# Five of six weight products of a unit and token block issued as two matmuls of 256 columns

## The chip, the cores and the metric

The kernel runs on one core of one Trainium2 chip. The metric is the time of one execution on the device in microseconds (us), and the median of several runs is compared. Every time below comes from such runs or from one execution that the hardware profiler recorded.

## The reference, cut to what matters

The computation is a decoder trunk of two layers on 256 tokens with a model width of 2048, all in 32-bit floats. Layer 0 has a combined input projection (2048 to 6160), stick-breaking attention beside gated linear attention, and an output projection (2048 to 2048). Layer 1 has a diagonal state-space mixer and a gated projection (2048 to 4096). Both layers end in a SwiGLU feed-forward part (2048 to 11264, then 5632 to 2048), and every part has norms before and after it:

```python
for layer in range(DEPTH):
    y = rms_norm(h, g[0])
    y = sb_gla_mixer(y, ...) if layer % 2 == 0 else s5_mixer(y, ...)
    h = h + rms_norm(y, g[1])
    y = swiglu_ffn(rms_norm(h, g[2]), w_ffn_in[layer], w_ffn_out[layer])
    h = h + rms_norm(y, g[3])
```

Nearly all of the arithmetic is the product of 256 tokens with these weight matrices, some 360 MB of weights that are each read once.

## The kernel before

**Splitting a product.** A weight product in full 32-bit precision is made of three products in the type fp32r, which TensorE streams at one pass. Activations and weights are each split into a high part and a low remainder; the kernel adds activation high times weight high, activation high times weight low, and activation low times weight high. ScalarE (ACT) makes the high part of a weight by a rounding copy and VectorE (DVE) makes the low part by a subtraction (`Stream.convert`, line 108).

**Tiles.** The output is made in blocks of 512 columns, and each block has two token blocks of 128 tokens, each of which adds up in one PSUM bank of 128 x 512 floats. Weights come from memory by the SP queue in chunks of 512 rows by 512 columns (1 MB); half a chunk, 256 rows, is a *unit*. `linear` (line 208) and `pairwise` (line 265) loop over the column blocks and, within one, over the units; for each unit they fetch its split weights (`ws.next`), call `products` (line 192) for token block 0 and for token block 1, and then let `pump` (line 171) issue some background work for DVE and ACT by the planner's costs.

**A call of `products`.** It handles one unit for one token block: two row blocks `kk` of 128 rows, and for each of them the three products of lines 203, 204 and 205. In the call of the matmul the activations (128 rows by 128 tokens) are the stationary operand, which TensorE has to load first (LDWEIGHTS, the engine PEld in the profile), and the weights (128 rows by 512 columns) stream past them. Each of these six matmuls has its own load. The first matmul of an output block carries the flag `start`, which clears the bank, and the last carries `stop`, after which ACT and DVE read the bank. A few chunks of layer 1 have no low part and go through plain 32-bit matmuls on line 198 instead.

**Order.** The schedule is written by hand: TensorE's instructions stand in the order in which the code issues them, and an instruction waits for what it reads. The converter runs `ahead` units (3 or 4) in front of TensorE. Between units the background work may put transposes or small matmuls of the mixers into TensorE's order (lines 337, 480, 734, 810, 923 to 954, 1233, 1414 to 1490).

**How many.** The stream holds 48 chunks of the input projection, 16 of the output projection, 176 and 88 of the feed-forward parts and 32 of the gated projection: 360 chunks, of which 4 go through line 198. The other 356 are 712 units. There are 92 column blocks (12, 4, 68 and 8), so 184 accumulations with one first and one last matmul each.

Of the kernel before, what the change touches and what calls it, by code (L numbers as in the profile page):

```python
# [159 lines left out]
class Kern:  # L160
# [31 lines left out]
    def products(self, ps, acts, tb, u, part):  # L192
        hi, lo = part
        mm = self.nc.tensor.matmul
        if lo is None:
            for kk in range(2):
                k = 2 * u + kk
                mm(ps, lhsT=self.whole[k][:, tb * 128:(tb + 1) * 128], rhs=hi[:, kk, :], start=(k == 0), stop=(k == len(acts) - 1))  # L198
            return
        for kk in range(2):  # L200
            k = 2 * u + kk
            xh, xl = (a[:, tb * 128:(tb + 1) * 128] for a in acts[k])
            mm(ps, lhsT=xh, rhs=hi[:, kk, :], start=(k == 0), stop=False)  # L203
            mm(ps, lhsT=xh, rhs=lo[:, kk, :], start=False, stop=False)  # L204
            mm(ps, lhsT=xl, rhs=hi[:, kk, :], start=False, stop=(k == len(acts) - 1))  # L205


    def linear(self, blocks, acts, evac, opening=None, mid=None, hooks=None, spare=None):
# [497 lines left out]
    def gla(self, rs):  # L706
# [86 lines left out]
        yield from self.need(256)  # L793
        mix = self.got.pop(256)
        yield from products(S[1], mix, mix, 0, 128, lambda o, p: nc.vector.tensor_copy(o, p))
        for li, b in enumerate((64, 32, 16, 8, 4, 2, 1)):
            yield from self.need(2 * b + 1)
# [805 lines left out]
```

## Time and profile before

| what | value |
|---|---|
| time, median of 3 runs | 2204.62 us (2203.36 to 2204.85) |
| the profiled execution's own time | 2204.35 us |
| its span, first to last instruction | 2202.6 us |
| mean granted TensorE clock | 0.996 |
| PE busy (matmul) | 2159.6 us, 98% of the span, 10672 instructions |
| PEld busy (loads of the stationary operand) | 1741.4 us, 79%, 10672 instructions |
| DVE busy | 1319.5 us, 60% |
| ACT busy | 974.3 us, 44% |
| mean rate of the DMA queues | 208 GB/s |

A matmul's row in the profile lasts longer than its share of the engine, because matmuls overlap in the pipeline: the row of a 512-column matmul is some 396 ns long, while the next begins some 232 ns after it. What a matmul costs is therefore read from the distance between starts. In a row, `128*128 128x512 f32` means 128 rows by 128 columns of stationary operand and 512 streamed columns; a plain 32-bit matmul appears as two rows, one for each of its passes. PEclk is the granted clock as a share of full speed.

### The profile page before, as it was taken

To read this page: it belongs to the slowest core of one execution; us is meant where nothing else is said; L and a number is where in the kernel's file an instruction comes from. 1 tells how busy PE (TensorE), PEld (TensorE's weight loads), DVE (VectorE), ACT (ScalarE), POOL (GpSimd) and SP (SyncE) were. 2 spreads that over 40 slices of the span, in tenths; PEclk is the share of its full clock that TensorE was granted. 3 is DMA by queue.
4 is the path that set the end of the run, shared out by engine and by line. 5 is a ranking of instruction groups with operands and counts; after the bars stand their busy time and mean duration, and the time that the engine had idled before them with its cause. 6 is when DMAs were issued, how large, how long until landed. Compare 5 with 4: busy or idle time off the path is not lost.

```text
span 2202.6 us, 26942 instructions
## 1 busy us (share of the span) xinstructions
PE 2159.6 (98%) x10672; PEld 1741.4 (79%) x10672; DVE 1319.5 (60%) x1913; ACT 974.3 (44%) x1222; POOL 7.1 (0%) x14
## 2 busy tenths in 40 slices
PE   8999999999999999999998899999999999999998
PEld 6888888788888888777786678878888888888886
DVE  4675654667777877875456864564544454444445
ACT  5454544463454444334344254464434444433433
POOL 0000000000000000000000000000000000000000
PEclk9999999999999999999999999999999999999999
DMA  7554454555687778988769865645555555555553
GB/s 230 171 176 156 159 173 155 206 190 175 202 268 236 241 221 267 300 275 275 238 214 349 305 209 185 213 170 176 195 183 191 191 173 190 174 206 174 191 172 134
DMA packets 261742, 457.42 MB, mean 208 GB/s; under 512 B 22736, under 2 KB 66016, under 8 KB 260720
## 3 DMA queue, kind: packets, MB, share of 16 engines
q1 hardware_dynamic: 260896, 450.99, 62.0%
q0 software_dynamic: 720, 4.72, 0.6%
q8 instruction: 83, 1.36, 0.2%
q14 instruction: 43, 0.35, 0.0%
HBM read 425.26 MB, written 30.41 MB: 207 GB/s over the span
## 4 chain that ended last, share of the span: by engine, by line
PE 94%; DVE 3%; ACT 1%; DMA 1%; issue 0%; SPq 0%; DVEq 0%; ACTq 0%
PE lin L203 29%; PE lin L205 29%; PE lin L204 29%; PE lin L198 1%; PE big L480 1%; DVE h L65 1%; DVE X L65 0%; PE big L810 0%; DVE wlo L65 0%; ACT xh L65 0%; PE big L1233 0%; PE big L205 0%; PE big L204 0%; PE big L203 0%; DVE xl L65 0%
## 5 line engine op out<-in xcount | busy, mean ns | idle before, releaser
L65 DVE TENSOR_TENSOR wlo<-wraw,whi 128x1024 fp32r<-128x1024 f32 x705 | 850.3, 1222 | 591.1 <-ACT whi L65 588.8
L65 ACT CAST whi<-wraw 128x1024 fp32r<-128x1024 f32 x705 | 725.3, 1051 | 670.7 <-PE lin L205 609.2
L203 PE MATMUL lin<-whi,xh 128*128 128x512 f32 x1984 | 790.6, 398 | 3.4 <-ACT xh L65 3.4
L204 PE MATMUL lin<-wlo,xh 128*128 128x512 f32 x1984 | 785.1, 396 | 3.0 <-DVE wlo L65 2.9
L205 PE MATMUL lin<-whi,xl 128*128 128x512 f32 x1984 | 784.9, 396 | 0.9 <-DVE xl L65 0.9
L203 PEld LDWEIGHTS lin<-whi,xh 128*128 128x128 f32 x1984 | 374.9, 189 | 91.2 <-ACT xh L65 4.0
L204 PEld LDWEIGHTS lin<-wlo,xh 128*128 128x128 f32 x1984 | 374.8, 189 | 90.4 <-DVE wlo L65 6.0
L205 PEld LDWEIGHTS lin<-whi,xl 128*128 128x128 f32 x1984 | 374.5, 189 | 88.7 <-DVE xl L65 2.2
L203 PE MATMUL lin<-whi,ah 128*128 128x512 f32 x680 | 270.0, 397 | 0.0
L205 PE MATMUL lin<-whi,al 128*128 128x512 f32 x680 | 268.9, 395 | 0.0
L204 PE MATMUL lin<-wlo,ah 128*128 128x512 f32 x680 | 268.9, 395 | 0.0
L203 PEld LDWEIGHTS lin<-whi,ah 128*128 128x128 f32 x680 | 128.1, 188 | 30.8 <-issue 1.2
L205 PEld LDWEIGHTS lin<-whi,al 128*128 128x128 f32 x680 | 128.1, 188 | 30.3
L204 PEld LDWEIGHTS lin<-wlo,ah 128*128 128x128 f32 x680 | 128.1, 188 | 30.0
L65 DVE SCALAR_TENSOR_TENSOR a<-lin,rs,a 128x512 f32<-128x512 f32 x44 | 31.0, 746 | 67.3 <-PE lin L205 67.3
L65 ACT ACTIVATE a<-lin,rs 128x512 f32<-128x512 f32 x44 | 27.9, 684 | 92.2 <-PE lin L205 92.2
L65 DVE TENSOR_TENSOR yg<-lin,yg 128x512 f32<-128x512 f32 x30 | 19.9, 687 | 52.1 <-PE lin L205 52.1
L65 ACT ACTIVATE junk<-yg 128x512 f32<-128x512 f32 x24 | 15.2, 632 | 74.1 <-DVE yg L65 74.1
L65 ACT CAST ah<-big 128x1024 fp32r<-128x1024 f32 x22 | 22.3, 1015 | 56.2 <-PE big L480 56.2
L65 DVE TENSOR_TENSOR al<-big,ah 128x1024 fp32r<-128x1024 f32 x22 | 26.9, 1223 | 17.1 <-ACT ah L65 17.1
L65 ACT ACTIVATE xh<-big,gT 128x128 fp32r<-128x128 f32 (+1 forms) x80 | 24.3, 394 | 21.5 <-PE big L337 16.9
L65 DVE SCALAR_TENSOR_TENSOR xl<-big,gT,xh 128x128 fp32r<-128x128 f32 (+1 forms) x80 | 24.5, 371 | 13.6 <-ACT xh L65 13.6
(323 smaller groups left out, 1287.1 us busy)
## 6 DMA issues: line engine op xcount, KB each, us to landing
wraw<-w_ffn_in SPq DMA_DIRECT2D x176, 1024.0 KB, 5.1
wraw<-w_ffn_out SPq DMA_DIRECT2D x88, 1024.0 KB, 5.5
wraw<-w_in SPq DMA_DIRECT2D x47, 1024.0 KB, 5.0
wraw<-w_glu SPq DMA_DIRECT2D x32, 1024.0 KB, 5.7
wraw<-w_out SPq DMA_DIRECT2D x16, 1024.0 KB, 5.1
e_d<-ed SPq DMA_DIRECT2D x64, 144.0 KB, 5.9
et<-e_d SPq DMA_DIRECT2D x16, 576.0 KB, 6.3
win_d<-win SPq DMA_DIRECT2D x32, 256.0 KB, 6.6
```

The source lines that it names most:

```text
L65: return f(*a, **k)
L198: mm(ps, lhsT=self.whole[k][:, tb * 128:(tb + 1) * 128], rhs=hi[:, kk, :], start=(k == 0), stop=(k == len(acts) - 1))
L203: mm(ps, lhsT=xh, rhs=hi[:, kk, :], start=(k == 0), stop=False)
L204: mm(ps, lhsT=xh, rhs=lo[:, kk, :], start=False, stop=False)
L205: mm(ps, lhsT=xl, rhs=hi[:, kk, :], start=False, stop=(k == len(acts) - 1))
L480: nc.tensor.transpose(p[:, tb, i, :], a[:, tb, i * 128:(i + 1) * 128], self.ident)
```

## The change

The three products of a row block become a list of terms, and each term is issued either whole (512 columns) or as two matmuls of 256 columns each, which write the two halves of the bank and stream the two halves of the weights. Both halves use the same stationary operand. Whole stay the first term of the first row block of a unit (`kk == 0 and i == 0`, which includes the one with `start`), and the matmul with `stop`. So a call issues 11 matmuls in place of 6, or 10 where it holds the last one of an accumulation. The order of the sums in each output element is the same. Loads, conversions, transfers, the reading of the banks and the plain 32-bit path on line 198 are as they were.

```diff
         for kk in range(2):
             k = 2 * u + kk
             xh, xl = (a[:, tb * 128:(tb + 1) * 128] for a in acts[k])
-            mm(ps, lhsT=xh, rhs=hi[:, kk, :], start=(k == 0), stop=False)
-            mm(ps, lhsT=xh, rhs=lo[:, kk, :], start=False, stop=False)
-            mm(ps, lhsT=xl, rhs=hi[:, kk, :], start=False, stop=(k == len(acts) - 1))
+            terms = ((xh, hi), (xh, lo), (xl, hi))
+            for i, (x, w) in enumerate(terms):
+                start, stop = k == 0 and i == 0, k == len(acts) - 1 and i == 2
+                whole = stop or (kk == 0 and i == 0)
+                for c in (slice(0, 512),) if whole else (slice(0, 256), slice(256, 512)):
+                    mm(ps[:, c], lhsT=x, rhs=w[:, kk, c], start=start, stop=stop)
```

## The prediction

> **What bounds the kernel now.** I read the page first: the busy shares, then the chain of work that ended last, then the costliest groups.
>
> ```profile
> span 2202.6 us, 26942 instructions
> PE 2159.6 (98%) x10672; PEld 1741.4 (79%) x10672; DVE 1319.5 (60%) x1913; ACT 974.3 (44%) x1222; POOL 7.1 (0%) x14
> PE 94%; DVE 3%; ACT 1%; DMA 1%; issue 0%; SPq 0%; DVEq 0%; ACTq 0%
> PE lin L203 29%; PE lin L205 29%; PE lin L204 29%; PE lin L198 1%; PE big L480 1%; DVE h L65 1%; DVE X L65 0%; PE big L810 0%; DVE wlo L65 0%; ACT xh L65 0%; PE big L1233 0%; PE big L205 0%; PE big L204 0%; PE big L203 0%; DVE xl L65 0%
> ```
>
> TensorE sets the end: 94% of the chain is PE, 87% of it the three lines of the change. So what matters is how fast TensorE passes from one matmul to the next. The timeline of TensorE and its loads shows that (start in us, length in us):
>
> ```profile
> 600.17 0.39 PE L203 MATMUL lin<-whi,xh 128*128 128x512 f32 x1
> 600.40 0.40 PE L204 MATMUL lin<-wlo,xh 128*128 128x512 f32 x1
> 600.40 0.19 PEld L205 LDWEIGHTS lin<-whi,xl 128*128 128x128 f32 x1
> 600.63 0.40 PE L205 MATMUL lin<-whi,xl 128*128 128x512 f32 x1
> 600.63 0.19 PEld L203 LDWEIGHTS lin<-whi,xh 128*128 128x128 f32 x1
> ...
> 611.33 0.39 PE L203 MATMUL lin<-whi,xh 128*128 128x512 f32 x1
> ```
>
> Line 203 starts at 600.17 and again at 611.33, 48 matmuls later (16 times the three lines in turn): 11.16 us / 48 = **232.5 ns** from one whole matmul to the next. The load of the next stationary operand starts together with the matmul before it (600.40, 600.63) and its row is 0.19 us long, so it is done before that matmul ends.
>
> The other engines leave room where the work is densest (busy us of PE, PEld, DVE and ACT, then PEclk, DMA share and GB/s):
>
> ```profile
> 480.00:1180.00 700.00, 700.00 (x3260) 562.97 (x3260) 487.12 (x838) 296.58 (x346) 0.29 (x1) 1.00 0.77 242
> 1440.00:2180.00 740.00, 738.05 (x3231) 598.86 (x3230) 364.56 (x366) 312.01 (x362) 0.53 (x1) 1.00 0.54 182
> ```
>
> In these two stretches DVE is busy for 487 of 700 us and 365 of 740, and the DMA engines for 0.77 and 0.54 of the time, so a TensorE that is a few per cent faster is still fed. Should one of them be late next, it is DVE, whose low part of a unit is made in one piece:
>
> ```profile
> L65 DVE TENSOR_TENSOR wlo<-wraw,whi 128x1024 fp32r<-128x1024 f32 x705 | 850.3, 1222 | 591.1 <-ACT whi L65 588.8
> ```
>
> That is 1.22 us for a unit on which TensorE works for 12 x 232.5 ns = 2.79 us, so it hides with room of more than half.
>
> **The change part by part.** A unit and token block has six products. The stream has 712 split units (356 chunks by 2) and two token blocks: 712 x 2 x 6 = 8544 whole matmuls. At 232.5 ns they fill 1986 us, 90% of the span, which agrees with the chain's 87%. Whole stay 1424 firsts (712 x 2) and 184 lasts (92 column blocks x 2): 8544 - 1424 - 184 = **6936 products are cut in two**. That removes 6936 matmuls of 512 columns and adds 13872 of 256, each with its own load of 128 columns; so 6936 loads are added too. One ns on a cut product is 6.94 us. No wait is added: a half reads the same tiles and the `stop` matmul, on which the readers of the bank wait, stays single.
>
> What one half costs is not in the trace as such: an fp32r matmul of 256 columns with 128 loaded columns. Three rows stand around it. The nearest in type and length is line 734, fp32r too and 256 columns, but with a load of 16 columns:
>
> ```profile
> L734 PE MATMUL big<-xh,wlr_split 128*16 128x256 f32 x32 | 5.7, 278 | 0.6 <-ACT wlr_split L65 0.4 <-DVE wlr_split L65 0.2
> 46.42 0.28 PE L734 MATMUL big<-xl,wlr_split 128*16 128x256 f32 x1
> ...
> 50.84 0.28 PE L734 MATMUL big<-xl,wlr_split 128*16 128x256 f32 x1
> ```
>
> The low product comes once in three there, so 13 x 3 = 39 matmuls lie between these two rows: 4.42 us / 39 = **113.3 ns**. Two of them are 226.7, which is 5.8 ns less than a whole one. The second row is the nearest in the load: line 810, a plain 32-bit product, whose passes of 128 columns run at half the rate and take as much stream as 256 columns of fp32r, each with a load of 128 columns. Beside it I put line 198, the same kind with 512 columns:
>
> ```profile
> 182.92 1.95 PE L810 MATMUL big<-qd,de 128*128 128x128 f32 x16
> 182.92 1.76 PEld L810 LDWEIGHTS big<-qd,de 128*128 128x128 f32 x15
> L810 PE MATMUL big<-qd,de x112: 273/276/276, 118.3 to 197.5; 128*128 128x128 f32 x112
> 1259.79 2.74 PE L198 MATMUL lin<-wraw,y 128*128 128x512 f32 x6
> L198 PE MATMUL lin<-wraw,y x64: 592/593/697, 1249.4 to 1281.8; 128*128 128x512 f32 x64
> ```
>
> Sixteen rows of line 810 in 1.95 us, the last 276 ns long: (1950 - 276) / 15 = **111.6 ns** from one to the next. So TensorE takes a load of 128 columns every 111.6 ns beside a stream of that length: the load fits under a half of 113.3 ns, with less than 2 ns to spare. Line 198: (2740 - 593) / 5 = 429.4 ns.
>
> Does the load slow the stream, so that twice as many loads cost more? One row speaks against it: a 512-column matmul behind which no load ran.
>
> ```profile
> 427.60 0.39 PE L204 MATMUL big<-hl,os 128*128 128x512 f32 x1
> 427.61 0.19 PEld L205 LDWEIGHTS big<-hl,os 128*128 128x128 f32 x1
> 427.83 0.40 PE L205 MATMUL big<-hl,os 128*128 128x512 f32 x1
> 429.22 0.42 PEld L337 LDWEIGHTS big<-ident,h 128*128 128x128 f32 x4 [1.43 <-DVE xl L65]
> ```
>
> The matmul of 427.83 has no load beside it until 429.22, and its row is 0.40 us, as long as that of 427.60, which has one. So the load is not what makes 512 columns cost more than twice 113.3 ns. What does, the trace does not say: the length itself, or the 128 output columns where line 734 has 16.
>
> The cost of a half is thus bounded from below by 111.6 ns (the load has no room under it), and from above by the case that all that a whole fp32r matmul has over its ideal is paid per instruction. Half of line 198's pass, 429.4 / 2 = 214.7, is that ideal for 512 columns; 232.5 - 214.7 = 17.8 ns is the surplus, and a half would be 107.35 + 17.8 = 125.2 ns. I take **114.0**: the row of the same type and length, 113.3, and 0.7 for a load that is tight against it (112 of 113). Two halves are 228.0, which is 4.5 ns less than 232.5; 6936 x 4.5 = **31 us** less. Nothing else enters the sum. The other terms at nothing: more instructions to hand out, since line 1233 hands out a pair of load and matmul every 25 ns, (650 - 279) / 15, and more to fetch, which is 1.36 of 457 MB moved:
>
> ```profile
> 1010.12 0.65 PE L1233 MATMUL big<-et 128*32 128x128 f32 x16
> L1233 PE MATMUL big<-et 128*32 128x128 f32 x256 | 10.3, 279 | 0.0
> DMA packets 261742, 457.42 MB, mean 208 GB/s; under 512 B 22736, under 2 KB 66016, under 8 KB 260720
> ...
> q8 instruction: 83, 1.36, 0.2%
> ```
>
> If hiding fails there, each of the 6936 pairs costs what it is late by. The sum stands against the profiled execution's own 2204.35 us (its span of 2202.6 and 1.75 around it): 2204.35 - 31.2 = 2173.1. The median of the runs is 0.27 us above that execution, so **2173 us** stands for both.
>
> A rule of the Trainium skill speaks against the change. TensorE: Matmul & The Clock Gate, section Back-to-back issue gap, gives 518 cycles for 512 columns and 262 for 256 at full clock, so by it two halves cost 6 cycles more than one, an estimate of 2.5 ns, or 17 us more in all (2222). The trace has 232.5 and 113.3 ns where that page has 216 and 109, so the excess that the page does not know is on the long matmul; the measurement decides, and the rule's sign lives on in the first rival.
>
> **The rivals.**
>
> *A fixed price per matmul* (slower). Four matmuls of 128 columns on line 810 are 446.4 ns, one of 512 on line 198 is 429.4: three more matmuls and loads cost 17.0 ns, 5.7 each. If fp32r streams at a rate of its own that goes by the column (232.5 for 512), a cut product costs 232.5 + 5.7: 6936 x 5.7 = 39 us more, 2243. It happens at the hand-over between two halves, and it decides from a half of 116.6 ns on. For it: both rows are firm, and a load that starts with the matmul before it has only the half's length. Against it: line 734 hands over 39 times at 113.3, less than half of 232.5. At the far end of the same place lies the whole surplus of 17.8 per matmul: 6936 x 17.8 = 123 us, 2328; line 734, with 6 ns over its ideal, speaks against that.
>
> *The rate goes by the column and the hand-over is free* (no change). If 2.2 columns per ns is simply what fp32r does with 128 output columns, a half is 116.25 and two are 232.5: 2204. For it: the row without a load is as long as the others, so the surplus sits in the stream. Against: 113.3 on line 734.
>
> *The change does more than the row* (faster still). With halves at 111.6, the bound of the load, the gain is 9.3 x 6936 = 65 us, 2140. Nothing shows fp32r streaming faster than line 734, so I give this little.
>
> **How the numbers follow.** My forecast, halves between 112.5 and 115.9 ns, has 0.50; its own range is 2153 to 2200. No change, within 0.2% (4.4 us, 0.3 ns on a half; about what a measurement of this kernel can tell), has 0.13. The fixed price at some 5.7 ns has 0.26, and its far end, towards 2328, 0.08. Still faster has 0.03. Together: faster 0.53, same 0.13, slower 0.34. The range goes down to 2150, which leaves out the last case, and up to 2290, which is 85.7 / 6.936 = 12.4 ns on a cut product or a half of 122.4 ns, well past the fixed price of 5.7 and short of its far end; with that end about 0.1 is left out in all, a little less than it might be, since no row shows the half itself.
>
> **What would show it.** In the changed kernel the groups of the split line have the form 128x256 with a mean near 278 ns, as on line 734 (near 282 if the rate goes by the column), and 13872 of them; two matmuls of 256 start 228 ns apart from the next two in the timeline. The load rows come 114 ns apart and PEld is busy for nearly all of the span. The whole matmuls stay at 232.5. PE waits and DVE's busy time stay as they are. The prediction is wrong if halves start over 116.25 ns apart; if then the load's rows start late, after the matmul before them, the load is the bound, and if the matmul rows are longer than 282 ns it is the stream.

## The result

The changed kernel is slower: 2229.5 us against 2204.49, medians of 4 runs each. The ratio is **1.0117**, 95% interval 1.0099 to 1.0134. That is 25.0 us more, or 25.0 / 6.936 = 3.6 ns on each of the 6936 cut products, where the prediction had 4.5 ns less. The profiled execution took 2227.84 us, 23.5 more than that of before.

The page of the changed kernel, busy shares and the chain's shares by engine, answers first how much work there is and what it hangs on:

```profile
span 2226.1 us, 40814 instructions
PE 2183.9 (98%) x17608; PEld 2072.6 (93%) x17608; DVE 1319.7 (59%) x1913; ACT 973.6 (44%) x1222; POOL 7.1 (0%) x14
PE 94%; DVE 2%; ACT 1%; issue 1%; DMA 1%; SPq 0%; DVEq 0%; ACTq 0%
```

17608 - 10672 = 6936 matmuls more, and 6936 loads more, so the count holds. DVE and ACT are as busy as before, and the chain is TensorE's to the same 94%. The two dense stretches show no more for DVE, ACT and the DMA engines to do than before (busy us of PE, PEld, DVE, ACT and POOL, then PEclk, DMA share and GB/s):

```profile
480.00:1180.00 700.00, 700.00 (x5562) 668.73 (x5560) 482.63 (x834) 294.44 (x343) 0.28 (x1) 1.00 0.75 238
1440.00:2180.00 740.00, 738.05 (x5697) 709.84 (x5696) 362.58 (x369) 310.31 (x358) 0.53 (x1) 1.00 0.55 185
```

The granted clock is 1.00 there in both kernels. The DMA share went from 0.77 to 0.75 in the first and from 0.54 to 0.55 in the second, so the transfers run no harder. Of the table of what PE waited for (us in all, times, longest), here are the longest waits and the largest on the changed line:

```profile
PE big L1393 <- ACT yg L65: 7.3, 2, 7.1
...
PE lin L1493 <- issue: 4.2, 2, 3.0
PE lin L208 <- DVE wlo L65: 2.5, 5, 0.8
```

Before, the wait in front of the same instruction (line 1490 there) was put down to DVE with 2.6 us, so it is 1.6 us longer; no other grew by more than 1.3. Over the whole table PE waited 32.6 us, and 33.8 before. The time is therefore not in the waits. The timeline has it (start, length in us; `x2` is a pair of halves):

```profile
599.89 0.40 PE L208 MATMUL lin<-whi,xh 128*128 128x512 f32 x1
599.89 0.42 PEld L208 LDWEIGHTS lin<-wlo,xh 128*128 128x128 f32 x2
600.12 0.40 PE L208 MATMUL lin<-wlo,xh 128*128 128x256 f32 x2
600.24 0.30 PEld L208 LDWEIGHTS lin<-whi,xl 128*128 128x128 f32 x2
600.36 0.39 PE L208 MATMUL lin<-whi,xl 128*128 128x256 f32 x2
...
601.30 0.40 PE L208 MATMUL lin<-whi,xh 128*128 128x512 f32 x1
...
611.19 0.40 PE L208 MATMUL lin<-whi,xh 128*128 128x512 f32 x1
```

The whole matmul opens each call, so 8 calls lie between 599.89 and 611.19: 11.30 us / 8 = 1412.5 ns for a call of 11 matmuls. Before, a call was 6 x 232.5 = 1395. The 17.5 ns between them are 3.5 ns for each of the five cut products; 6936 x 3.5 = 24 us, close to the loss of the profiled execution (23.5) and of the medians (25.0). The ten halves take 601.30 - 600.12 = 1.18 us, **118.0 ns each**, and over all starts of the trace a half is followed after 117.9 ns on average. No load is late: the one for the half of 600.24 is issued with the start of that half's predecessor, and the next pair with the half of 600.24.

### The profile page after: what moved, and what is told of

Read it like the earlier page. It is cut to its first block, busy times and chain, and to the rows that moved or that the text cites. A ratio compares the mean times of both kernels' runs of the same rounds, so it can differ in the third digit from the quotient of the medians.

```text
span 2226.1 us, 40814 instructions
## 1 busy us (share of the span) xinstructions
PE 2183.9 (98%) x17608; PEld 2072.6 (93%) x17608; DVE 1319.7 (59%) x1913; ACT 973.6 (44%) x1222; POOL 7.1 (0%) x14
## 4 chain that ended last, share of the span: by engine, by line
PE 94%; DVE 2%; ACT 1%; issue 1%; DMA 1%; SPq 0%; DVEq 0%; ACTq 0%
PE lin L208 87%; PE big L208 1%; PE lin L198 1%; PE big L483 1%; DVE h L65 0%; PE big L813 0%; ACT xh L65 0%; PE big L1236 0%; DVE wlo L65 0%; DVE xl L65 0%; PE big L340 0%; ACT whi L65 0%; PE big L827 0%; PE big L737 0%; DMA wraw<-w_in 0%
## 5 line engine op out<-in xcount | busy, mean ns | idle before, releaser
L208 PE MATMUL lin<-whi,xh 128*128 128x256 f32 (+1 forms) x2976 | 800.6, 324 | 2.2 <-ACT xh L65 2.2
L208 PE MATMUL lin<-wlo,xh 128*128 128x256 f32 x3968 | 793.6, 281 | 2.6 <-DVE wlo L65 2.5
L208 PE MATMUL lin<-whi,xl 128*128 128x256 f32 (+1 forms) x3842 | 783.5, 282 | 0.8 <-DVE xl L65 0.8
L208 PEld LDWEIGHTS lin<-wlo,xh 128*128 128x128 f32 x3968 | 679.9, 188 | 57.4 <-DVE wlo L65 5.0
L208 PEld LDWEIGHTS lin<-whi,xl 128*128 128x128 f32 x3842 | 593.5, 188 | 1.5 <-DVE xl L65 1.5
L208 PEld LDWEIGHTS lin<-whi,xh 128*128 128x128 f32 x2976 | 486.8, 188 | 5.9 <-ACT xh L65 2.8
L208 PE MATMUL lin<-whi,ah 128*128 128x256 f32 (+1 forms) x1020 | 272.2, 321 | 0.0
L208 PE MATMUL lin<-wlo,ah 128*128 128x256 f32 x1360 | 270.9, 280 | 0.0
L208 PE MATMUL lin<-whi,al 128*128 128x256 f32 (+1 forms) x1314 | 269.0, 283 | 0.0
L208 PEld LDWEIGHTS lin<-wlo,ah 128*128 128x128 f32 x1360 | 232.6, 188 | 17.8
L65 DVE TENSOR_TENSOR al<-big,ah 128x1024 fp32r<-128x1024 f32 x22 | 26.9, 1223 | 17.5 <-ACT ah L65 17.5
```

The source lines that it names most:

```text
L65: return f(*a, **k)
L208: mm(ps[:, c], lhsT=x, rhs=w[:, kk, c], start=start, stop=stop)
```

## The experiments

Two kinds of kernel were run. Those whose names begin with m issue streams of matmuls by themselves; they leave out the whole computation of the reference. The others are the kernel with an edit. A stream's pitch, the distance from start to start, is worked out from its one row in the timeline as (length of the row - length of its last matmul) / (count - 1). The last matmul's length, from the groups by tile, is 388 to 401 ns for a whole one, 276 to 283 ns for a half of fp32r. Since the timeline rounds to 0.01 us, pitches given to a tenth come from the unrounded starts.

### Streams alone (m1_streams)

```python
def seg(name, load, cuts, count, lhs=x, rhs=w, ...):      # 4 banks in turn, one per segment
    for c in range(count):
        for a, b in cuts:                                 # whole: (0,512); half: (0,256), (256,512)
            nc.tensor.matmul(p[0:load, a:b], lhsT=lhs[:, c % 16, 0:load], rhs=rhs[:, c % 4, a:b], ...)
```

> This kernel leaves out the whole computation (it copies x to the output) and runs streams of back-to-back matmuls alone, one kind after the other, with no other engine at work; read is the distance between starts. Two theories for the half of 118 ns in the changed kernel. STREAM: fp32r with 128 output columns streams at 2.2 columns per ns and each matmul adds 1 to 4 ns; the load is hidden. LOAD: a half waits for the load of its 128 columns, which can start only with the matmul before it. Load 128: whole 232, half 117 to 118 by both. Load 64, half: 113 by LOAD (the load is half as long), between 113 and 118 by STREAM. Load 16, whole: 226 (twice line 734) by STREAM if the output columns set the rate, 232 if they do not. 384 and 128 columns in turn with a load of 128: 235 to 240 a product by STREAM alone, 175 + 111 = 286 if the load of 109 to 112 has to fit under the 128. 128 columns with a load of 128: 109 to 112 by LOAD, 62 by STREAM alone. Zero data in place of random: unchanged, 232 and 118, unless the rate hangs on the data (then down to 215 and 109). Plain fp32 passes: 429, 216, 110 as in the kernel before.

The timeline of that run; in the tile names `load` is the width of the load and `cut` that of the stream, `same` uses one stationary operand for all, `plain` is plain 32-bit:

```profile
31.72 11.04 PE L45 MATMUL load128cut512t<-w,x 128*128 128x512 f32 x48
42.60 11.67 PE L45 MATMUL load128cut256t<-w,x 128*128 128x256 f32 x96
54.11 11.28 PE L45 MATMUL load16cut512t<-w,x 128*16 128x512 f32 x48
65.23 11.05 PE L45 MATMUL load16cut256t<-w,x 128*16 128x256 f32 x96
76.12 11.20 PE L45 MATMUL load64cut512t<-w,x 128*64 128x512 f32 x48
87.15 11.05 PE L45 MATMUL load64cut256t<-w,x 128*64 128x256 f32 x96
98.04 13.87 PE L45 MATMUL load128cut384x128t<-w,x 128*128 128x384 f32 x96
...
139.20 11.68 PE L45 MATMUL zerocut256t<-z 128*128 128x256 f32 x96
183.38 11.68 PE L45 MATMUL samecut256t<-w,x 128*128 128x256 f32 x96
194.90 10.46 PE L45 MATMUL plaincut512t<-wr,h 128*128 128x512 f32 x24
205.20 10.52 PE L45 MATMUL plaincut256t<-wr,h 128*128 128x256 f32 x48
215.56 10.88 PE L45 MATMUL plaincut128t<-wr,h 128*128 128x128 f32 x96
```

The second row is the operation that the trace of before did not show: (11.67 - 0.283) / 95 = **120 ns** for a half with a load of 128 columns. With a load of 16 or 64 it is (11.05 - 0.276) / 95 = 113.4. So the prediction's 113.3 from line 734 was the price of a half with a small load, and the load of 128 columns adds 6.6 ns here. Neither the data nor the operand matter: zeros and one stationary operand for all give the same 120.

The row of 98.04 has each product cut into 384 and 128 columns instead. From the unrounded starts such a product costs 285.5 ns, 59 more than a whole one. The expectation had 286 for a load that has to fit under the 128 columns and 235 to 240 for a price of the stream, so this speaks for the load.

The first row is the second surprise: a whole matmul costs (11.04 - 0.389) / 47 = 226.6 here, not 232.5 as in the kernel. The plain ones give 429, 216 and 112. Cutting a plain pass of 512 in two thus costs 2 x 215.8 - 429.2 = 2.4 ns, in four 4 x 111.7 - 429.2 = 17.6: the price appears when the stream comes down to about the length of the load, 112 ns, and is not the same at every cut.

### All six products, and one (e_six, e_one)

```diff
-                whole = stop or (kk == 0 and i == 0)
+                whole = start or stop                            # e_six: 8176 products cut
+                whole = stop or not (kk == 0 and i == 1)         # e_one: 1424 products cut
```

> As the changed kernel, but of the six products only those with start or stop stay whole, so 1240 more are cut: 8176 in all. By one price per cut (25 us over 6936 cuts, 3.6 ns each) 29.5 us over the kernel before, 2234. By the halves and wholes of the changed kernel's trace (a half 117.9, a whole between halves 237) about the same as the changed kernel, 2228, since the wholes between halves are as dear as two halves.

> As the changed kernel, but of the six products only the second of the first row block (activation high by weight low) is cut, 1424 in all. By one price per cut of 3.6 ns: 5 us over the kernel before, 2209.6. If a cut is paid at the change from whole to halves (a whole between halves is 237 and not 232.5) and not by its number: 1424 x (4.5 + 3.3) = 11 us, 2216.

e_six took 2238.14 us against 2204.62, ratio 1.0150 (1.0133 to 1.0167): 33.5 us over 8176 cuts, 4.1 ns each. e_one took 2210.46 against the same, ratio 1.0025 (1.0015 to 1.0035): 5.8 us over 1424 cuts, 4.1 ns each. Both lie nearest to the expectation of one price per cut (2234 and 2209.6), a little above it. The loss grows with the number of cut products, at 3.6 to 4.1 ns whether one, five or six in a call are cut. So it is not that the odd whole one among halves breaks a rhythm, nor a cost per call.

### A narrower load in the kernel (e_load64, e_whole64)

```diff
                 whole = stop or (kk == 0 and i == 0)
-                for c in (slice(0, 512),) if whole else (slice(0, 256), slice(256, 512)):
-                    mm(ps[:, c], lhsT=x, rhs=w[:, kk, c], start=start, stop=stop)
+                for c in ...:                # e_load64: halves as in the change; e_whole64: (slice(0, 512),)
+                    t = 128 if whole else 64
+                    mm(ps[0:t, c], lhsT=x[:, 0:t], rhs=w[:, kk, c], start=start, stop=stop)
```

Both leave out the products of 64 of the 128 tokens of a block, in the five products that the change cuts.

> The changed kernel, except that the five cut products of a call load 64 columns in place of 128, and so leave out the sums of tokens 64 to 127 of each token block; number and length of the matmuls are those of the change. LOAD (a half of 256 columns cannot hide a load of 128): halves at 113.3 as in the streams alone, a cut product 226.7 against 232.5, 6936 x 5.8 = 40 us under the kernel before, 2164. STREAM (a price per matmul or per column whatever is loaded): as the changed kernel, 2228.

> The kernel before, except that the same five products load 64 columns in place of 128 and leave out the sums of tokens 64 to 127; all matmuls have 512 columns. It is the control of the run before: in the streams alone a whole matmul costs 230.0 with a load of 64 and 226.7 with 128, so both theories expect the time of the kernel before within 20 us, 2190 to 2225, and what the halves are worth with a short load is the difference between the two runs.

Whole with a load of 64: 2193.36 us against 2205.81, ratio 0.9945 (0.9928 to 0.9962). Cut with a load of 64: 2211.86, ratio 1.0032 (1.0020 to 1.0044). The cut costs 18.5 us at this width, 2.7 ns each, less than the 25.0 at 128 columns, but not the gain that the 113.4 ns of the streams alone had promised (2164 in the expectation). So either the width was not the cause, or the streams alone differed from the kernel in something else; the 232.5 ns of a whole one said the latter.

### The kernel's own order and its neighbours (m2_like)

```python
for i, (l, r) in enumerate(((a, hi), (a, lo), (b, hi))):      # a, b: slices of xh, xl as in the kernel
    for c in (half if cut(kk, i) and not start and not stop else whole):
        nc.tensor.matmul(pt[:, tb, c], lhsT=l, rhs=r[:, k % 4, c], start=start, stop=stop)
# the same once with ACT, once with DVE, once with DMA busy beside it
```

> This kernel leaves out the whole computation and runs streams of matmuls alone. Why does a whole matmul cost 232.5 in the kernel and 226.7 in the streams alone? If it is the order of the operands (high and low parts in turn, two banks, a stationary tile of 256 columns), the stream that is built like the kernel's calls shows 232; if it is the other engines or DMA, only the streams with ACT, DVE or DMA busy do. For the halves: like the change (five of six cut) 117 to 120 by LOAD with both, six of six cut 119 to 120.

The timeline shows the alternation of high and low part, of which the first and last of 48 matmuls stand here:

```profile
65.30 0.39 PE L65 MATMUL hilot<-hi,x 128*128 128x512 f32 x1
...
75.95 0.39 PE L65 MATMUL hilot<-hi,x 128*128 128x512 f32 x1
```

(75.95 - 65.30) / 47 = 226.6, and the stream from the 256-column wide stationary tile, 48 matmuls in 11.04 us, gives (11.04 - 0.389) / 47 = 226.6 too. All whole ones, in the order of a call too, started 680 ns per three (226.7 each), also while ACT, DVE or the DMA engines worked. Cut as in the change, halves were followed after 118.8 ns on average, with all six products cut after 119.8. Neither order, nor banks, nor neighbours make the 232.5. In all these streams both operands happened to start at addresses of the same remainder by 256 bytes, which led to the next two runs.

### Where the tiles lie (m3_places, m4_offsets)

```python
arena = pool.tile([128, 42 * 1024], F32R)      # both operands are cut out of one large tile
nc.tensor.matmul(p[:, a:b], lhsT=arena[:, la:la + 128], rhs=arena[:, ra + a:ra + b], ...)
# m3: la, ra at 5 x 5 far places, then at the kernel's own; m4: the start of one moved by 64 bytes at a time
```

> This kernel leaves out the whole computation and runs streams of whole matmuls with a load of 128 columns, the streamed tile and the stationary tile at five places each of a partition's memory, 0 to 150 KB behind the start of one array. If the place of the operands is what makes a whole matmul 226.7 in the streams alone and 232.5 in the kernels, the stream and load at the places of the kernel's weight and activation tiles (wholek) show 231 to 234 and some of the 25 pairs differ from 226.7. If the place does not matter, all of them show 226.7 and a half 120.

> This kernel leaves out the whole computation. Where the run before put the operands at the kernel's own places, a whole matmul cost 232.5 with the kernel's own pattern, and 226.7 at 25 places that all start 128 bytes behind a multiple of 1024. So the start within a block of 512 to 2048 bytes would set it. Here the streamed tile starts at every 64 bytes from 0 to 1984 behind a multiple of 1024 with the stationary tile at 0, and the stationary tile at every 64 bytes up to 448 with the streamed tile at 0 and at 384. If only the streamed tile's start counts, its sweep moves and the other does not; if only their distance counts, both move alike; if neither, all show 226.7. A half with a load of 128: 113 to 120, and below 116.25 at some start if the kernel's halves suffer from the start and not from the load.

m3_places, timeline: the first of the 25 pairs of places, and the kernel's own place (`k`), whole and cut:

```profile
30.11 9.23 PE L43 MATMUL streamaloadat<-arena 128*128 128x512 f32 x40
...
256.79 9.46 PE L43 MATMUL wholekt<-arena 128*128 128x512 f32 x40
266.08 9.66 PE L43 MATMUL halfkt<-arena 128*128 128x256 f32 x80
```

All 25 pairs have the first row's (9.23 - 0.389) / 39 = 226.7. At the kernel's place it is (9.46 - 0.393) / 39 = **232.5**, the number of the kernel, with nothing else running. Halves there are (9.66 - 0.281) / 79 = 118.7. m4_offsets names the variable; timeline rows, where `stream` and `load` are the bytes by which the two starts were moved:

```profile
32.08 5.60 PE L42 MATMUL wholestream0load0t<-arena 128*128 128x512 f32 x24
37.52 5.67 PE L42 MATMUL wholestream64load0t<-arena 128*128 128x512 f32 x24
43.02 5.75 PE L42 MATMUL wholestream128load0t<-arena 128*128 128x512 f32 x24
48.61 5.76 PE L42 MATMUL wholestream192load0t<-arena 128*128 128x512 f32 x24
...
286.83 5.92 PE L42 MATMUL halfstream0load0t<-arena 128*128 128x256 f32 x48
292.58 5.85 PE L42 MATMUL halfstream0load128t<-arena 128*128 128x256 f32 x48
```

From the unrounded starts, without the first four of each stream and averaged over all places, whole matmuls cost 226.8, 228.8, 232.3 and 233.4 ns. This repeated with a period of 256 bytes in all 32 positions of the streamed tile and in both sweeps of the stationary one: for whole matmuls with a load of 128 columns only the distance (streamed start - stationary start) modulo 256 decides. Halves go the other way, 119.9 at distance 0 and 118.5 at 128: (5.92 - 0.283) / 47 and (5.85 - 0.281) / 47. In the kernel the split weights start at remainder 128; `xh`, `xl` and the `ah`, `al` of layer 0 at 0, so they stand at distance 128, and the `ah`, `al` of layer 1 at 192, distance 192. In its trace, pitches averaged over six matmuls lie for the middle half at 232.3 to 233.3 for the former, and at 233.3 for the latter.

### Distance and width together (m5_loads)

Edit: the streams of m4_offsets with `lhsT=arena[:, la:la + load]` for loads of 16 to 128 columns at four distances, and 60 products of which every sixth is whole.

> This kernel leaves out the whole computation: streams of wholes and halves at the four distances 0, 64, 128 and 192 bytes with loads of 16 to 128 columns, and the change's mix (one whole, ten halves). LOAD: at every distance a half is 113.3 with 16 columns and dearer by 3 to 7 ns from some width between 64 and 128 on, where the load no longer fits. If instead the number of matmuls or the distance sets the half's price, the width of the load does not change it. The mix at distance 128, the kernel's, should give the changed kernel's 1412 ns for a call of eleven.

The timeline at the kernel's distance of 128 bytes (`columns` is the width of the load):

```profile
166.01 5.61 PE L42 MATMUL halfstream128columns16t<-arena 128*16 128x256 f32 x48
171.46 5.61 PE L42 MATMUL halfstream128columns32t<-arena 128*32 128x256 f32 x48
176.90 5.76 PE L42 MATMUL halfstream128columns64t<-arena 128*64 128x256 f32 x48
182.50 5.92 PE L42 MATMUL halfstream128columns96t<-arena 128*96 128x256 f32 x48
188.26 5.82 PE L42 MATMUL halfstream128columns112t<-arena 128*112 128x256 f32 x48
193.91 5.86 PE L42 MATMUL halfstream128columns128t<-arena 128*128 128x256 f32 x48
```

That is 113.5, 113.3, 116.7, 120.0, 117.8 and 118.7 ns. At this distance a load of 64 already costs a half 3.4 ns. In e_load64 the halves on a tile at this distance (`ah` of layer 0) take 116.9 ns, as here; m1_streams, at distance 0, could not show it. The price does not simply grow with the width. A whole one with a load of 64 has 229.3 here, so a cut there costs 2 x 116.7 - 229.3 = 4.1 ns.

The width of the load is also the number of rows of the bank that a matmul writes, and no run changes one without the other. But at one width the price of a half moves with the distance (with 96 columns 116.0, 113.3, 120.0 and 113.3 ns at 0, 64, 128 and 192), and the rows written are the same there. So the rows written alone do not set it. The mix of one whole and ten halves took 1413 ns per call at distance 128, the changed kernel's 1412.5: matmuls and loads alone make its whole price.

### The tiles moved, in the kernel (e_place, e_place_five)

```diff
+    def pad(self, pool, n):
+        self.nc.gpsimd.memset(pool.tile([128, n], F32, name=f"pad{self.uid()}"), 0.0)
...
         self.hss = [...]
+        self.pad(pool, 32)           # and pad(..., 48) first in the pools mix0, s5a and ffn
```

e_place is the kernel before with these small unused tiles, which put weights and activations at the same remainder by 256 bytes; e_place_five has the change as well.

> The kernel before, with four small pads between its tiles so that the weight tiles and the activation tiles start at the same place within 256 bytes (before: 128 bytes apart for the first activations and one feed-forward tile, 192 for the others). PLACE (the distance of the streamed from the stationary tile within 256 bytes sets what a whole matmul costs: 226.7 at 0, 228.9 at 64, 232.3 at 128, 233.3 at 192): 5.8 to 6.6 ns less for each of 8544 matmuls, 50 to 56 us less, 2150 to 2156. If the other engines or the length of the run make the 232.5: unchanged, 2204.

> The changed kernel with the same pads. In the streams alone a half with a load of 128 costs 120.0 at distance 0 and 118.7 at 128. PLACE: a cut product 240 against a whole of 226.7, 6936 x 13.3 = 92 us over the kernel with pads alone, and 6936 x (240 - 235.8) - 1608 x 6 = 20 us over the changed kernel, 2250. If the halves gain from the pads as the wholes do: 2180.

e_place took **2158.89 us** against 2205.31, ratio **0.9790** (0.9776 to 0.9805), 46.4 us less: 5.4 ns on each of 8544 whole matmuls, a little short of the 5.8 to 6.6 expected. Its timeline:

```profile
600.06 0.39 PE L203 MATMUL lin<-whi,xh 128*128 128x512 f32 x1
...
601.87 0.39 PE L205 MATMUL lin<-whi,xl 128*128 128x512 f32 x1
```

Eight matmuls in 601.87 - 600.06 = 1.81 us are 226 ns each. e_place_five took 2243.01, ratio 1.0172 (1.0155 to 1.0189). With the tiles there, the same change costs 84.1 us, 12.1 ns on each cut product; the streams alone say 2 x 120.0 - 226.7 = 13.3. So the price of the change hangs on where the tiles lie, and the kernel before was a mild case: its whole matmuls were dear already.

### The load at 32 columns (e_load32, e_whole32)

The edits of e_load64 and e_whole64 with `t = 128 if whole else 32`; the five products leave out 96 of the 128 tokens.

> As the run with loads of 64 columns on the cut products, with 32 (it leaves out the sums of tokens 32 to 127 of each token block in those products). Alone, halves at the kernel's distances cost 113.3 with loads of 16 or 32 and 116.7 to 118.7 with 64 or 128. LOAD: halves come down from 117 to 113.3, a cut product to 226.7, 13872 x 3.8 = 52 us under the run with 64 columns, 2160. If the halves stay at 117 inside the kernel whatever is loaded, 2212 as with 64, and the load is not what they pay for there.

> The control for the cut products with loads of 32 columns: the same five products load 32 columns (and leave out the sums of tokens 32 to 127 of each token block), but stay whole. With loads of 128 the cut costs 25 us, with 64 it costs 18. LOAD: with 32 it costs nothing or gains, so this run is 2183 or more. If every cut costs 3 to 4 ns whatever is loaded, this run is 25 us under the cut one, 2158.

Cut: 2183.27 us against 2204.28, ratio 0.9908 (0.9892 to 0.9925). Whole: 2187.62 against 2204.97, ratio 0.9921 (0.9903 to 0.9939). The intervals overlap: with a load of 32 columns the cut costs nothing that can be told. The cut run lies between its two expectations (2160 and 2212): its halves are followed after 115.3 ns on average, not 113.3, and two of them match the 230.7 ns of a whole one with that load in e_whole32. The three pairs side by side, same work in both columns of a row:

| columns loaded in the five products | whole, us | cut, us | the cut costs |
|---|---|---|---|
| 128 (before, after) | 2204.5 | 2229.5 | +25.0 |
| 64 | 2193.4 | 2211.9 | +18.5 |
| 32 | 2187.6 | 2183.3 | -4.3, not told from 0 |

Rows 2 and 3 issue as many matmuls, loads and instructions as row 1, as the page of e_load32 and that of e_whole32 show, in this order:

```profile
span 2178.6 us, 40814 instructions
PE 2134.1 (98%) x17608; PEld 1828.7 (84%) x17608; DVE 1317.4 (60%) x1913; ACT 974.4 (45%) x1222; POOL 7.1 (0%) x14
```

```profile
span 2186.3 us, 26942 instructions
PE 2142.5 (98%) x10672; PEld 1180.8 (54%) x10672; DVE 1319.5 (60%) x1913; ACT 973.3 (45%) x1222; POOL 7.1 (0%) x14
```

Only the width of the load, and with it the rows written and the part of the computation, differs. So the loss comes from the wide load beside the short stream, and not from the number of instructions.

## Why the prediction was wrong

**What bounds the kernel, and the count: right.** TensorE sets the end in both, 6936 products were cut, and no other engine, transfer or wait gained weight worth more than 2 us. A loss of 3.5 ns on 6936 products accounts for the difference, as the prediction's sum was built.

**The price of a half: wrong, and this alone turned the sign.** The step that failed is "I take 114.0: the row of the same type and length, 113.3, and 0.7 for a load that is tight against it". A half measured 117.9 in the kernel; alone it took 118.5 to 118.7 at distance 128 and 117.8 at 192, the kernel's two distances. With 117.9, 2 x 117.9 - 232.5 = 3.3 ns per cut, 23 us, on the right side; the prediction turned over at 116.25. The row of line 734 itself was read rightly: m5_loads has 113.3 to 113.5 for a load of 16 at three of four distances. At distance 0 it has 116.7, where m1_streams had 113.4; no run explains that.

**"The load fits under a half, with less than 2 ns to spare": the reading behind that step.** Line 810 shows that a load of 128 columns and a stream of equal length go on at 111.6 ns. From that I took the longer of the two as the price of the pair. The runs say otherwise: a load whose own pitch is 111.6 and a stream whose own is 113.3 make 117.8 to 120.0 together. The prediction named this row as a lower bound, and as that it holds; its upper bound, 125.2, holds too. Within them the value was chosen by the row nearest in type and length, when the width of the load was the dimension that mattered.

**"The load is not what makes 512 columns cost more": half right.** That the surplus of the whole, 232.5 against twice 113.3, was due to the length or to the 128 output columns is refuted: at distance 0 a whole one with 128 output columns costs 226.7, exactly twice 113.3. It is the distance of the two tiles. But the row quoted for it, one matmul of 0.40 us without a load beside it, was the length of one row, and lengths of rows (389 to 397 ns in the streams alone) hardly follow pitches. Why that row is no shorter stays open.

**Nothing for more instructions and more fetches: right.** e_load32 issues 40814 instructions as well, and is not slower than e_whole32.

**The rivals.** Of the three, the fixed price per matmul was nearest in time (5.7 ns per cut product and 2243, against 3.6 and 2229.5), and "decides from a half of 116.6 ns on" was met. As a mechanism it fell: the price is about 0 with a load of 32, 12.1 with the tiles at distance 0, and on the plain 32-bit rows that it came from, a first cut costs 2.4 ns and not 5.7. No change by a rate that goes by the column fell as well. The rule of the Trainium skill (TensorE: Matmul & The Clock Gate, section Back-to-back issue gap), by which a cut costs 6 cycles, an estimate of 2.5 ns, had the sign and came to 2222, nearer still. On the plain 32-bit passes of m1_streams these runs agree with it: a first cut costs 2.4 ns. For fp32r it does not hold as a price of each matmul: two halves with loads of 32 columns take 226.7 ns, which is what one whole takes at its best, and with loads of 128 at distance 0 the cut costs 13.3. So its nearness here is luck.

**The signs that I named.** The halves' rows came out between the two values that I set, 278 and 282 ns, so that they told nothing:

```profile
L208 PE MATMUL lin<-wlo,xh 128*128 128x256 f32 x3968 | 793.6, 281 | 2.6 <-DVE wlo L65 2.5
L208 PE MATMUL lin<-whi,xl 128*128 128x256 f32 x3716 | 734.1, 279 | 0.8 <-DVE xl L65 0.8
```

The loads were not issued late either, and yet the load is the cause: by the test "if then the load's rows start late, after the matmul before them, the load is the bound" it would have been missed. It slows the pair without showing as a wait. The whole matmuls did not quite stay at 232.5: those left in front of halves are followed after 236.3 ns on average, 3.8 ns more on each of some 1400, which the prediction had put at nothing.

**What stays open.** Why a wide load slows a short stream, and why the distance modulo 256 bytes decides how much, was not shown; that both operands are fetched from one memory and get in each other's way there fits both, but it is only argued. With narrow loads, kernel and streams alone do not agree everywhere. The halves of e_load32 start 114 to 117 ns apart by tile, where 113.3 came out alone. Those of e_load64 on a tile at distance 192 (`ah` of layer 1) take 118.6 where m5_loads has 113.3. A stream that mixes wholes with a load of 128 and halves with a narrower one would bear on this; of the two written for it, m6_mix and m6_mixes, neither gave a time.

## What to carry to other kernels

Price a TensorE instruction by a row that agrees in type, in streamed columns and in the width of its load; if no row does, take a stream whose length nears that of its load as dearer than either alone, as it was here; a value just above the smaller neighbour is no safe middle. Where TensorE bounds a kernel, read the pitch from starts, compare it with the best pitch of the same form, and look at how the start addresses of streamed and stationary tiles stand to each other: here some bytes of padding were worth 2.1%, more than the 1.4% that was forecast for the change (31 of 2204). Halving a stream needs a reason other than speed: with loads of 128 and 64 columns it cost time, with 32 it gained nothing that can be told.

## What the runs showed of the hardware that was not expected

- **The distance of two tiles.** A 512-column fp32r matmul with a load of 128 columns costs 226.7, 228.8, 232.3 to 232.8 or 233.4 ns as the streamed tile starts 0, 64, 128 or 192 bytes behind the stationary one, modulo 256. In the kernel, going to 0 took 2205.31 us to 2158.89. The Trainium skill (SBUF — State Buffer, section Who interferes with whom) lists a read port each for streamed and loaded operand, independent of each other, and says that TensorE never waits on anyone. These runs agree as far as other engines go, since pitches stayed at 226.7 beside busy ACT, DVE and DMA engines; between TensorE's own two operands they show up to 3%, and the measurement decides.
- **Wide loads beside short streams.** Alone, a 256-column fp32r matmul costs 113.3 to 113.6 ns with a load of 32 columns at every distance, 117.8 to 120.0 with 128, and with 64 or 96 columns either, as the distance has it (113.3 or 116.7; 113.3 to 120.0).
- **Whole matmuls with a small load are not the cheapest.** With a load of 16 columns they cost 231.4 to 231.7 ns at all four distances, more than with 128 columns at distance 0 (226.7). No run explains it.
- **128 columns.** With a load of 32, fp32r streams of 128 columns start 60.0 ns apart; with a load of 128, 111.6, the pace of the plain 128-column passes with the same load. There the load alone sets the pace.
